# Another order of column tiles and of the steps that run beside them in a hybrid block of pooling, gated DeltaNet, latent attention and MLP

## The chip, the core and the metric

The kernel runs on one core of a Trainium2 chip. Its time is device microseconds of one execution; the kernel before took 1226.1, 1227.61 and 1230.46 us in three runs, median 1227.61. A profile was taken of one execution.

## The reference

One block of depth 1 on x of 1024 rows and 1024 columns, all in float32. One projection gives all inputs of three mixers, whose outputs are joined, projected and added to x; an MLP with squared ReLU follows.

```python
h = rms_norm(x, attn_norm[l])
proj = h @ w_in[l]
xa, qkv, z, b, a, c_q, c_kv, k_pe = jnp.split(proj, offsets, axis=-1)
y_a = pool_mixer(xa, ...)         # window means of 2, 4, 8, 16 rows, minus xa, small product per group
y_b = gated_deltanet(qkv, z, b, a, ...)   # 4 heads of 128
y_c = mla_attention(c_q, c_kv, k_pe, ...) # 4 heads, causal softmax
x = x + jnp.concatenate([y_a, y_b, y_c], axis=-1) @ w_out[l]
h = rms_norm(x, mlp_norm[l])
x = x + jnp.square(jax.nn.relu(h @ w_up[l])) @ w_down[l]
```

The change touches the pooling mixer's projection and the DeltaNet. Its queries, keys and values go through a causal convolution of four taps and silu; per chunk of rows a unit lower triangular system is solved, and then a state of 128x128 per head is carried from chunk to chunk:

```python
sol = lax.linalg.triangular_solve(a_strict, rhs, left_side=True, lower=True, unit_diagonal=True)
def step(state, inp):
    u_i, w_i, qd_i, kd_i, at_i, gl_i = inp
    v_new = u_i - jnp.einsum("bhck,bhkv->bhcv", w_i, state)
    o = jnp.einsum("bhck,bhkv->bhcv", qd_i, state) + jnp.einsum("bhij,bhjv->bhiv", at_i, v_new)
    state = state * gl_i[..., None, None] + jnp.einsum("bhck,bhcv->bhkv", kd_i, v_new)
    return state, o
```

## The kernel before, in words

The kernel takes chunks of 128 rows, eight of them. The input projection is cut into column tiles of 128 columns: 0 and 1 feed the pooling mixer, 2 to 5 the queries of the four heads, 6 to 9 the keys, 10 to 13 the values, 14 to 17 the gates. `proj_tile` works a tile in two halves of 512 rows; each half is 24 products of 128x128 by 128x512 (8 slices of the input times 3 terms of a split into a high and a low part, L123 to L125) into one PSUM bank. `tile_order` says whose weights are fetched ahead; the second operand of `load_w` says whether VectorE (`V`) or GpSimd (`G`) makes the low part of the weights (L116).

Everything else of the DeltaNet is written as generators that wait in queues (`side`, `slow`, `ahead`) and are advanced by `pump` once per half tile: n steps of `side`, m of `slow`. What a half tile has left for later (`later`) runs after the next half's products. Instructions are then set in order on each engine by a scheduler with a model of its own, so that the program's order is a wish and the order on an engine is what counts.

The parts of the DeltaNet, with the names that the rows use:
- `conv_silu` (L503 on ScalarE, three L506 and, in second halves, three L508 on VectorE, L512 on ScalarE, L514 on VectorE) is the convolution of a half tile of keys, queries or values.
- `lanes` inverts all 32x32 diagonal blocks of all heads and chunks at once, 128 of them, one in each partition: 31 pairs of L591 and L593 on VectorE, each dependent on the one before. A transposed copy is made by ScalarE (L595), and both go to DRAM (L596, L597), from where they are read back in block form.
- `levels(h)` builds the inverse of each 128x128 system of head h out of 32x32 blocks. It transposes the keys (L524, copies L725), fetches blocks (L741 to L752), and has five steps of eight small products, one for each chunk (`bat`, L758), with a copy behind each (L765 to L778).
- `chains(a, b)` is the recurrence of two heads. A step of a chunk: state products (L818, L819), the rest of the right side on VectorE (L821), the solve (L828), a scaled copy on VectorE (L832), the state's update (L839, then L844 on VectorE), the output (L847, L851). Every four chunks the norm, a scaling on ScalarE (L796), transposes (L801) and the gating (L803).
- The gates are made into `zs` by L716 and L717, the mixer's outputs copied by L657, the values transposed by L704, the products of queries and keys L685 and L688.

Before the change the tiles run: gates 0 and 1, queries 0, values 0, queries 1, values 1, the two mixer tiles, queries 2, values 2, queries 3, values 3, then the first halves of gates 2 and 3 and their second halves beside the first attention work. `lanes` was put in `side` ahead of the gates. `heads(0, 1)` enters `side` after values 1: the levels of two heads in turns, then their recurrence. `heads(2, 3)` enters after values 3.

Of the kernel before, what the change touches and what calls it, by code (L numbers as in the profile page):

```python
# [37 lines left out]
YU = 20  # L38
LAG = 2
OFF = 2  # L40
SIDE = 7
LANE = 4
BANKS = {"mm": 4, "sm": 2, "ch": 2, "s2": 2}
WINDOWS = (2, 4, 8, 16)
# [19 lines left out]
def block_kernel(ctx, tc, x, x_t, params, positions, attn_norm, w_tiles, w_g, w_qb, w_kvb, w_out,  # L64
# [14 lines left out]
    V, A, G, PE = nc.vector, nc.scalar, nc.gpsimd, nc.tensor  # L79
# [365 lines left out]
    def load_w(src, shape=(P, KD, P), eng=None):  # L445
        raw = S(shape, "raw", 3)
        nc.sync.dma_start(raw, src)
        hi, lo = S(shape, "w", 4, F32R), S(shape, "w", 4, F32R)
        split(hi, lo, raw, eng)
        return hi, lo  # L450
# [18 lines left out]
        while slow or side or ahead:  # L469
            pump(1, 1, 1)  # L470

    tile_order = [6, 7, 8, 9, 14, 15, 2, 10, 3, 11, 0, 1, 4, 12, 5, 13, 16, 17]
    loaded = {}

    def prefetch(ct):
        if ct not in loaded:
            loaded[ct] = load_w(w_tiles[ct], eng=V if ct in (15, 2, 10, 3, 11) else G)

    def proj_tile(ct, use, n=0, m=1, halves=(0, 1), tag="mm", between=None):
        prefetch(ct)  # L480
        hi, lo = loaded[ct]
        nxt = tile_order.index(ct) + 1
        for hf in halves:
            if hf == halves[-1] and nxt < len(tile_order):
                prefetch(tile_order[nxt])
            pm = MM(tag)
            due = later[:]
            del later[:]
            for k in range(KD):
                mm3(pm, hi[:, k, :], lo[:, k, :], ht_hi[hf][:, k, :], ht_lo[hf][:, k, :], k == 0, k == KD - 1)  # L490
            use(hf, pm)
            for f in due:
                f()
            pump(n, m)
            if between and hf == halves[0]:
                between()
# [121 lines left out]
    def pool(i, xa):  # L618
        cur = xa
        shifts = (1, 2) if i == 0 else (1, 2, 4, 8)  # L620
        for n, s in enumerate(shifts):
            nxt = U(s="xs")
            rows = slice(0, P) if n < len(shifts) - 1 else slice(64, P)
            if n == len(shifts) - 1:
                A.copy(nxt[0:64, :], cur[0:64, :])
            G.tensor_copy(nxt[rows, 0:s], cur[rows, 0:s])
            G.tensor_tensor(nxt[rows, s:], cur[rows, s:], cur[rows, :1024 - s], op=ALU.add)
            cur = nxt
            yield
        yp = U(s="yp")  # L630
        G.tensor_tensor(cur[:, 0:16], cur[:, 0:16], rcp[:, i, :], op=ALU.mult)
        G.tensor_tensor(yp[:, 0:16], cur[:, 0:16], xa[:, 0:16], op=ALU.subtract)
        V.scalar_tensor_tensor(yp[:, 16:], cur[:, 16:], rw[:, i:i + 1], xa[:, 16:], op0=ALU.mult, op1=ALU.subtract)
        nc.sync.dma_start(y_dram[i], yp)
        yield
# [17 lines left out]
    def mixer(i):  # L653
        xa = XA[i] = U(s="xa")

        def use_x(hf, pm):
            A.copy(xa[:, hf * 512:(hf + 1) * 512], pm)  # L657

        return i, use_x
# [16 lines left out]
    def query_key(h):  # L676
        qt = QT[h]
        transposed(qt, square_sums(ssq[:, h, :]))
        V.tensor_scalar(tq[:, h, :], ssq[:, h, :], EPS, EPS * 128.0, op0=ALU.add, op1=ALU.mult)
        att = E[h]  # L680
        for b in range(2):
            pk = MM("sm")
            for j in range(4):
                c = 4 * b + j
                PE.matmul(pk[:, j * P:(j + 1) * P], KT[h][:, c * P:(c + 1) * P], qt[:, c * P:(c + 1) * P], start=True, stop=True)  # L685
            for j in range(4):
                c = 4 * b + j
                V.scalar_tensor_tensor(att[:, c, :], pk[:, j * P:(j + 1) * P], c2[:, h, c:c + 1], att[:, c, :], op0=ALU.mult, op1=ALU.mult)  # L688

    def values(h):  # L690
        vs = VS[h] = U((P, NC, P), s="vs")
        vt = [None, None]

        def half(hf):
            vt[hf] = W()
            return vt[hf]

        def use_v(hf):
            later.append(lambda: turn_v(hf))

        def turn_v(hf):
            pt = MM("sm")
            for j in range(4):
                PE.transpose(pt[:, j * P:(j + 1) * P], vt[hf][:, j * P:(j + 1) * P], ident)  # L704
            for j in range(4):
                c = 4 * hf + j
                A.activation(vs[:, c, :], pt[:, j * P:(j + 1) * P], AF.Copy, scale=sk[:, h, c:c + 1])

        return 10 + h, conv_silu(8 + h, half, use_v)
# [11 lines left out]
    def levels(h):  # L721
        kk = KK[h] = U((P, NC, P), s="ktok")

        def use_k(b, pt):
            A.copy(kk[:, 4 * b:4 * b + 4, :].rearrange("p a b -> p (a b)"), pt)  # L725

        transposed(KT[h], use_k)
        tt2 = TT2[h] = U((P, NC, P), s="tt2")
        w1, w2, w3 = U((P, 2, NC, 64), s="w1"), U((P, 2, NC, 64), s="w2"), C((64, 2, NC, 32), "lv", 3)
        a_pair, w_pair = w1[0:64, 0], w1[0:64, 1]  # L730
        a_half, t_half, w_half = w2[0:64, 0], w2[0:64, 1], w2[64:128, 0]
        t_even, tt_odd = w3[:, 0], w3[:, 1]
        a_src = a_dram[h].rearrange("j (c i) -> j c i", c=NC)

        def block(q, b):
            return t_dram[q, h * 32 + b * 8:h * 32 + b * 8 + 8].rearrange("c (i j) -> i c j", i=32)

        G.memset(w1[0:64].rearrange("p a b c -> p (a b c)"), 0.0)
        for p_ in range(2):
            rows = slice(32 * p_, 32 * p_ + 32)  # L740
            nc.scalar.dma_start(a_pair[rows, :, rows], a_src[64 * p_:64 * p_ + 32, :, 64 * p_ + 32:64 * p_ + 64])  # L741
            nc.sync.dma_start(t_even[rows], block(0, 2 * p_))
            nc.sync.dma_start(tt_odd[rows], block(1, 2 * p_ + 1))
        G.memset(t_half[0:32, :, 32:64], 0.0)
        nc.scalar.dma_start(a_half, a_src[0:64, :, 64:128])
        for b in range(2):
            rows = slice(32 * b, 32 * b + 32)
            nc.sync.dma_start(t_half[rows, :, rows], block(0, b))
        G.memset(tt2.rearrange("p a b -> p (a b)"), 0.0)
        for b in range(4):  # L750
            rows = slice(32 * b, 32 * b + 32)
            nc.sync.dma_start(tt2[rows, :, rows], block(1, b))  # L752
        yield

        def bat(n, w, lhs, rhs):
            pa = MM(LVB)[0:n, 0:NC * w].rearrange("p (a b) -> p a b", a=NC)
            for c in range(NC):
                PE.matmul(pa[:, c, :], lhs[:, c, :], rhs[:, c, :], start=True, stop=True)  # L758
            return pa


        pa = bat(64, 32, a_pair, t_even)
        for p_ in range(2):
            rows = slice(32 * p_, 32 * p_ + 32)
            A.activation(w_pair[rows, :, rows], pa[rows], AF.Copy, scale=-1.0)  # L765
        yield
        pa = bat(32, 32, tt_odd[0:32], w_pair[0:32, :, 0:32])
        A.copy(t_half[32:64, :, 0:32], pa)
        yield
        pa = bat(64, 32, w_pair, tt_odd)  # L770
        for p_ in range(2):
            A.copy(tt2[64 * p_:64 * p_ + 32, :, 64 * p_ + 32:64 * p_ + 64], pa[32 * p_:32 * p_ + 32])
        yield
        pa = bat(64, 64, a_half, t_half)
        A.activation(w_half, pa, AF.Copy, scale=-1.0)
        yield
        pa = bat(64, 64, w_half, tt2[64:128, :, 64:128])
        V.tensor_copy(tt2[0:64, :, 64:128], pa)  # L778
        yield
        if h == 1:  # L780
            tap("TT2", tt2.rearrange("p a b -> p (a b)"))
# [82 lines left out]
                split(Y[2 + h][b][:, 0, :], Y[2 + h][b][:, 1, :], QT[h][:, 512 * b:512 * b + 512], YENG)  # L864
                yield

    def heads(*hs):
        gens = [levels(h) for h in hs]
        while gens:
            for g in list(gens):  # L870
                try:
                    next(g)
                    yield
                except StopIteration:
                    gens.remove(g)
        yield from chains(*hs)

    dn_half = const((P, 1), "dn_half")
    V.tensor_scalar(dn_half, pv("dn_norm"), 0.5, None, op0=ALU.mult)
    for h in range(2):  # L880
        proj_tile(*gate(h), LANE, 2)
        if h == 0:
            later.append(key_scales)
    for h in range(H):
        n = LANE if h < 2 else SIDE
        queries(h, n)
        proj_tile(*values(h), n, between=lambda: later.append(lambda: query_key(h)))
        if h == 1:
            drain()
            side.append(heads(0, 1))  # L890
            for i in range(2):
                proj_tile(*mixer(i), SIDE, 3)
                slow.append(pool(i, XA[i]))
    side.append(heads(2, 3))
    ends = [gate(h) for h in (2, 3)]
    for z in ends:
        proj_tile(*z, SIDE, halves=(0,))
# [409 lines left out]
    n = 0  # L1307
# [266 lines left out]
```

## Time and profile before

| | |
|---|---|
| median of three runs | 1227.61 us (1226.1 to 1230.46) |
| profiled execution | 1227.87 us |
| its span from the first to the last instruction | 1226.2 us |
| PE (products) busy | 1174.1 us, 96% |
| DVE (VectorE) busy | 849.6 us, 69% |
| ACT (ScalarE) busy | 582.1 us, 47% |
| POOL (GpSimd) busy | 266.7 us, 22% |
| mean granted clock of TensorE | 0.976 |

Busy time is the time in which at least one instruction of the engine ran; matmuls are pipelined, so that a matmul with a duration of 0.39 us is followed by the next after 0.227 us. The granted clock is the share of full speed that TensorE was given: 1.00 is 2.4 GHz and 0.50 is 1.2 GHz; a mean over a window between these says that both levels occurred in it.

### The profile page before, as it was taken

The numbers are of one execution on the slowest core, as the hardware profiler recorded it, in microseconds if no ns is written. First come the engines' busy times: TensorE is split into PE (matmuls) and PEld (weight loads), VectorE is DVE, ScalarE is ACT, GpSimd is POOL, SyncE is SP. The second block draws the span as 40 slices with busy tenths as digits, with TensorE's granted clock in tenths as the row PEclk, the third lists the DMA queues.
The fourth block names the chain that finished last, engine by engine and source line by source line (L and its number), as shares of the span: only waits on it lengthen the run. The fifth ranks groups of instructions, "written<-read, shape, count | busy, mean of one in ns | idle before, by whom it ended". The sixth has DMA issues, their size and how long they took to land.

```text
span 1226.2 us, 16233 instructions
## 1 busy us (share of the span) xinstructions
PE 1174.1 (96%) x5802; PEld 968.5 (79%) x5802; DVE 849.6 (69%) x1484; ACT 582.1 (47%) x1220; POOL 266.7 (22%) x309
## 2 busy tenths in 40 slices
PE   5999999899999889999899999999999999999998
PEld 5967777787778678788687788888888888888887
DVE  7676649627835877537698767667669897786863
ACT  6455434434644677524265455454554433333330
POOL 0135540232220326200423423424310000000000
PEclk9999999979998989999799999999999999999999
DMA  6101331320121211462125443443469964443302
GB/s 258 56 31 74 125 112 39 87 53 31 54 51 43 78 36 35 141 254 89 67 69 189 163 153 139 163 156 145 155 248 356 350 221 156 136 137 103 102 26 96
DMA packets 85696, 152.60 MB, mean 124 GB/s; under 512 B 25456, under 2 KB 28656, under 8 KB 85616
## 3 DMA queue, kind: packets, MB, share of 16 engines
q1 hardware_dynamic: 76624, 144.23, 33.3%
q10 hardware_dynamic: 8992, 7.34, 1.9%
q8 instruction: 46, 0.75, 0.2%
q14 instruction: 34, 0.28, 0.1%
HBM read 105.41 MB, written 46.14 MB: 124 GB/s over the span
## 4 chain that ended last, share of the span: by engine, by line
PE 75%; DVE 14%; ACT 4%; issue 3%; POOL 2%; DMA 1%; SPq 0%; DVEq 0%; ACTq 0%; POOLq 0%
PE mm L1449 14%; PE mm L1205 12%; PE sm L1205 6%; PE ch L1449 5%; PE sm L1449 5%; PE mm L125 4%; PE mm L124 4%; PE mm L123 4%; PE ch L1205 3%; DVE t2k L506 2%; PE sm L758 2%; PE ch L125 1%; DVE wop L116 1%; PE ch L123 1%; PE ch L124 1%
## 5 line engine op out<-in xcount | busy, mean ns | idle before, releaser
L1449 PE MATMUL mm<-dop,dop 128*128 128x512 f32 x768 | 176.0, 389 | 0.0
L1449 PEld LDWEIGHTS mm<-dop,dop 128*128 128x128 f32 x768 | 144.2, 188 | 29.9
L1205 PE MATMUL mm<-H,wop 128*128 128x512 f32 x576 | 141.5, 398 | 3.3 <-DVE uo L1273 2.7
L1205 PEld LDWEIGHTS mm<-H,wop 128*128 128x128 f32 x576 | 110.1, 192 | 28.1 <-DVE uo L1273 3.7
L115 ACT CAST dop<-wdr 128x1024 fp32r<-128x1024 f32 x48 | 50.4, 1050 | 151.2 <-PE mm L1449 62.9
L123 PE MATMUL mm<-H,w 128*128 128x512 f32 x288 | 118.7, 412 | 2.5 <-DVE zs L717 2.5
L125 PE MATMUL mm<-H,w 128*128 128x512 f32 x288 | 117.6, 408 | 0.0
L124 PE MATMUL mm<-H,w 128*128 128x512 f32 x288 | 117.3, 407 | 0.0
L1205 PE MATMUL sm<-op,wop 128*128 128x512 f32 x384 | 92.4, 389 | 1.4 <-ACT p L1271 1.4
L1205 PEld LDWEIGHTS sm<-op,wop 128*128 128x128 f32 x384 | 72.0, 188 | 16.8 <-ACT p L1271 1.9
L116 DVE TENSOR_TENSOR dop<-wdr,dop 128x1024 fp32r<-128x1024 f32 x48 | 58.6, 1222 | 31.2 <-ACT dop L115 31.2
L1295 ACT ACTIVATE uo<-uo 128x512 f32<-128x512 f32 x48 | 30.3, 631 | 98.3 <-DVE uo L1273 56.5
L1242 POOL TENSOR_TENSOR s<-upr 128x512 f32<-128x512 f32 x16 | 25.7, 1605 | 217.2 <-DVE uo L1231 98.2
L1449 PE MATMUL sm<-dop,dop 128*128 128x512 f32 x288 | 67.4, 389 | 0.0
L1449 PE MATMUL ch<-dop,dop 128*128 128x512 f32 x288 | 67.4, 389 | 0.0
L116 POOL TENSOR_TENSOR w<-raw,w 128x1024 fp32r<-128x1024 f32 x13 | 31.9, 2453 | 158.4 <-ACT w L115 158.4
L116 DVE TENSOR_TENSOR wop<-s,wop 128x512 fp32r<-128x512 f32 x64 | 45.7, 729 | 29.3 <-ACT wop L115 29.3
L123 PEld LDWEIGHTS mm<-H,w 128*128 128x128 f32 x288 | 55.5, 193 | 11.9 <-DVE zs L717 2.9
L506 DVE SCALAR_TENSOR_TENSOR t2k<-mm,cw,t2k 128x511 f32<-128x511 f32 (+2 forms) x72 | 53.5, 743 | 15.4 <-ACT t2k L503 15.1
L125 PEld LDWEIGHTS mm<-H,w 128*128 128x128 f32 x288 | 55.4, 192 | 10.1
L116 DVE TENSOR_TENSOR dop<-H,dop 128x1024 fp32r<-128x1024 f32 x52 | 63.2, 1216 | 0.0
L124 PEld LDWEIGHTS mm<-H,w 128*128 128x128 f32 x288 | 55.7, 193 | 9.3
(390 smaller groups left out, 2644.7 us busy)
## 6 DMA issues: line engine op xcount, KB each, us to landing
H<-u_dram SPq DMA_DIRECT2D x52, 512.0 KB, 4.3
upr<-in_w_up_dram SPq DMA_DIRECT2D x38, 512.0 KB, 4.0
u_dram<-t SPq DMA_DIRECT2D x64, 256.0 KB, 2.0
wdr<-in_w_down_dram SPq DMA_DIRECT2D x32, 512.0 KB, 7.7
u_dram<-uo SPq DMA_DIRECT2D x48, 256.0 KB, 2.0
raw<-in_w_tiles_dram SPq DMA_DIRECT2D x18, 512.0 KB, 3.4
wor<-in_w_out_dram SPq DMA_DIRECT2D x10, 512.0 KB, 8.4
x<-in_x_dram SPq DMA_DIRECT2D x8, 512.0 KB, 3.5
```

Source lines behind the costliest of these rows:

```text
L115: A.copy(hi, src)
L116: (eng or V).tensor_tensor(lo, src, f32(hi), op=ALU.subtract)
L123: PE.matmul(o, ah, bh, start=first, stop=False)
L124: PE.matmul(o, ah, bl, start=False, stop=False)
L125: PE.matmul(o, al, bh, start=False, stop=last)
L506: V.scalar_tensor_tensor(acc[:, s:], pm[:, :512 - s], w, acc[:, s:], op0=ALU.mult, op1=ALU.add)
L758: PE.matmul(pa[:, c, :], lhs[:, c, :], rhs[:, c, :], start=True, stop=True)
L1205: PE.matmul(o, x_, y_, start=(first and j == 0 and q == 0), stop=(j == 3 and q == 2), skip_group_check=True)
L1242: G.tensor_tensor(v.s12[:, 0], a21, a22, op=ALU.add)
L1295: A.activation(o, o, AF.Relu)
L1449: PE.matmul(o, x_[:, cs_], y_, start=(q in (0, 1, 3) and i == 0 and e == 0), stop=(i == GP - 1 and e == 2), skip_group_check=True)
```

## The change

The two mixer tiles move in front of queries 0, right behind gates 0 and 1, with `lanes` beside them; after them the program finishes what is left of `lanes`. Their weights are now split on VectorE. `heads` goes: `blocks` runs the levels one head after the other, and the recurrence is queued by itself. `blocks(0, 1)` is in `side` during queries and values 0 and 1, two steps per half tile; `chains(0, 1)` and `blocks(2, 3)` during queries and values 2 and 3; `chains(2, 3)` after those. `SIDE`, the steps per half tile from queries 2 on, is 8 for 7.

```diff
-SIDE = 7
+SIDE = 8
-    tile_order = [6, 7, 8, 9, 14, 15, 2, 10, 3, 11, 0, 1, 4, 12, 5, 13, 16, 17]
+    tile_order = [6, 7, 8, 9, 14, 15, 0, 1, 2, 10, 3, 11, 4, 12, 5, 13, 16, 17]
-            loaded[ct] = load_w(w_tiles[ct], eng=V if ct in (15, 2, 10, 3, 11) else G)
+            loaded[ct] = load_w(w_tiles[ct], eng=V if ct in (15, 0, 1, 2, 10, 3, 11) else G)
-    def heads(*hs):
-        gens = [levels(h) for h in hs]
-        while gens:
-            for g in list(gens):
-                try:
-                    next(g)
-                    yield
-                except StopIteration:
-                    gens.remove(g)
-        yield from chains(*hs)
+    def blocks(*hs):
+        for h in hs:
+            yield from levels(h)
...
+    for i in range(2):
+        proj_tile(*mixer(i), LANE, 2)
+    while side:
+        step(side, 1)
+    side.append(blocks(0, 1))
     for h in range(H):
-        n = LANE if h < 2 else SIDE
+        n = 2 if h < 2 else SIDE
         queries(h, n)
-        proj_tile(*values(h), n, between=lambda: later.append(lambda: query_key(h)))
+        proj_tile(*values(h), n, 3, between=lambda: later.append(lambda: query_key(h)))
         if h == 1:
             drain()
-            side.append(heads(0, 1))
-            for i in range(2):
-                proj_tile(*mixer(i), SIDE, 3)
-                slow.append(pool(i, XA[i]))
-    side.append(heads(2, 3))
+            side.append(chains(0, 1))
+            side.append(blocks(2, 3))
+            slow.extend(pool(i, XA[i]) for i in range(2))
+    side.append(chains(2, 3))
```

How this moves the engines' orders is shown at three places. On VectorE, the lanes. Before, early in queries 0 (the two tiles `mm_` are halves of queries 0):

```order
L591 TENSOR_TENSOR lt_1813<-lanes_741,tl_1807 128x87
L508 SCALAR_TENSOR_TENSOR t2k_2030<-carry_1956,cw,t2k_2030 128x1
L593 TENSOR_TENSOR tl_1807<-tl_1807,lt_1813 128x29x3
L506 SCALAR_TENSOR_TENSOR t2k_2030<-mm_2005,cw,t2k_2030 128x510
L591 TENSOR_TENSOR lt_1813<-lanes_741,tl_1807 128x112
L508 SCALAR_TENSOR_TENSOR t2k_2030<-carry_1956,cw,t2k_2030 128x2
L593 TENSOR_TENSOR tl_1807<-tl_1807,lt_1813 128x28x4
```

After, the same pairs, which now stand beside the mixer's tiles:

```order
L591 TENSOR_TENSOR lt_1813<-lanes_741,tl_1807 128x87
L593 TENSOR_TENSOR tl_1807<-tl_1807,lt_1813 128x29x3
L591 TENSOR_TENSOR lt_1813<-lanes_741,tl_1807 128x112
L593 TENSOR_TENSOR tl_1807<-tl_1807,lt_1813 128x28x4
L591 TENSOR_TENSOR lt_1813<-lanes_741,tl_1807 128x135
L593 TENSOR_TENSOR tl_1807<-tl_1807,lt_1813 128x27x5
```

The convolutions between the pairs are gone; the first one of queries 0 now stands behind 43 of the 62 lane instructions.

On TensorE, the block products of heads 0 and 1. Before, in the second half of the second mixer tile (`mm_2772`; the `sm_` tiles are outputs of `bat`, of two heads in turns, and the last row is the first product of the recurrence):

```order
L758 MATMUL sm_2534<-lv_2506,w_408_2504 64x32 x8
L758 MATMUL sm_2545<-w_401_2471,lv_2473 32x32 x8
L124 MATMUL mm_2772<-H_101,w_2578 128x512
L125 MATMUL mm_2772<-H_99,w_2579 128x512
L758 MATMUL sm_2555<-w_408_2504,lv_2506 32x32 x8
L758 MATMUL sm_2565<-lv_2473,w_401_2471 64x32 x8
L758 MATMUL sm_2608<-lv_2506,w_408_2504 64x32 x8
L123 MATMUL mm_2772<-H_99,w_2578 128x512
L758 MATMUL sm_2619<-w_402_2472 64x64 x8
L758 MATMUL sm_2629<-w_409_2505 64x64 x8
L758 MATMUL sm_2639<-tt_400_2470,w_402_2472 64x64 x8
L758 MATMUL sm_2649<-tt_407_2503,w_409_2505 64x64 x8
```

After, head 0 alone, in the first half of queries 1 (`mm_2449`):

```order
L758 MATMUL sm_2175<-lv_2158,w_340_2156 64x32 x8
L124 MATMUL mm_2449<-H_100,w_2308 128x512
L125 MATMUL mm_2449<-H_98,w_2309 128x512
L123 MATMUL mm_2449<-H_98,w_2308 128x512
L124 MATMUL mm_2449<-H_100,w_2308 128x512
L125 MATMUL mm_2449<-H_98,w_2309 128x512
L123 MATMUL mm_2449<-H_98,w_2308 128x512
L758 MATMUL sm_2228<-w_340_2156,lv_2158 32x32 x8
L758 MATMUL sm_2238<-lv_2158,w_340_2156 64x32 x8
L758 MATMUL sm_2286<-w_341_2157 64x64 x8
L124 MATMUL mm_2449<-H_100,w_2308 128x512
```

The five steps of head 0 stand four and more half tiles earlier in the row of tiles, with 6 and 9 matmuls between them; the fifth follows in the second half of queries 1.

On TensorE, the start of the second recurrence. Before, the last block products of heads 2 and 3 and c0 stand early in a second half of a gate tile (`mm_3905`), with a whole half tile behind it:

```order
L758 MATMUL sm_3818<-tt_693_3653,w_695_3655 64x64 x8
L758 MATMUL sm_3828<-tt_700_3686,w_702_3688 64x64 x8
L828 MATMUL ch_3841<-vs_3063,tt_693_3653 128x128
...
L818 MATMUL ch_3891<-st_3866,kt_1235 128x128
L819 MATMUL ch_3891<-st_3866,qt_2851 128x128
L818 MATMUL ch_3898<-st_3875,kt_1488 128x128
L819 MATMUL ch_3898<-st_3875,qt_3312 128x128
L123 MATMUL mm_3905<-H_99,w_3500 128x512
L124 MATMUL mm_3905<-H_101,w_3500 128x512
L125 MATMUL mm_3905<-H_99,w_3501 128x512
```

After, head 3's last block product stands in the last half tile (`mm_4211`), whose last matmul comes after c1 (L914 and L925 are the attention's transposes, L917 and L928 in the kernel before):

```order
L758 MATMUL sm_3800<-tt_697_3693,w_699_3695 64x64 x8
...
L828 MATMUL ch_3819<-vs_3433,tt_697_3693 128x128
...
L818 MATMUL ch_3871<-st_3827,kt_1235 128x128
L819 MATMUL ch_3871<-st_3827,qt_2709 128x128
L925 MATMUL sm_4106<-ident,t2k_4104 96x128 x2
L914 MATMUL sm_4138<-ident,raw_4135 96x128
L818 MATMUL ch_3878<-st_3836,kt_1488 128x128
L819 MATMUL ch_3878<-st_3836,qt_3227 128x128
L914 MATMUL sm_4138<-ident,raw_4135 96x128 x3
L125 MATMUL mm_4211<-H_99,w_3729 128x512
```

Behind c1 stand 33 matmuls of the gates' tiles before, and one after.

## Rows read from the trace of the kernel before

**Rows 1.** The page: busy us (share of the span) and instructions.

```profile
PE 1174.1 (96%) x5802; PEld 968.5 (79%) x5802; DVE 849.6 (69%) x1484; ACT 582.1 (47%) x1220; POOL 266.7 (22%) x309
```

**Rows 2.** Windows: length, busy PE, PEld, DVE, ACT, POOL, granted clock, DMA share, GB/s.

```profile
200.00:220.00 20.00, 19.90 (x98) 16.34 (x97) 19.33 (x52) 7.96 (x24) 2.40 (x1) 1.00 0.08 27
220.00:240.00 20.00, 16.11 (x81) 13.38 (x80) 13.65 (x36) 9.52 (x28) 4.50 (x4) 0.91 0.36 102
...
400.00:420.00 20.00, 17.80 (x111) 14.30 (x111) 17.78 (x50) 15.91 (x57) 7.42 (x16) 1.00 0.19 62
420.00:440.00 20.00, 13.44 (x60) 9.42 (x58) 12.52 (x34) 11.88 (x34) 3.93 (x3) 0.74 0.22 73
```

**Rows 3.** Waits of PE, 160 to 450 us: us in total, times, longest.

```profile
PE ch L801 <- ACT lv L796: 5.8, 2, 3.8
PE sm L704 <- DVE t2k L514: 4.6, 2, 3.9
...
PE ch L847 <- DVE st L844: 1.5, 3, 1.0
...
PE sm L685 <- ACT junk L541: 0.6, 1, 0.6
```

**Rows 4.** Short windows in which the clock is low, columns as in rows 2.

```profile
232.00:236.00 4.00, 4.00 (x16) 3.20 (x14) 1.31 (x3) 3.20 (x16) 0.00 (x0) 0.66 0.37 57
254.00:256.00 2.00, 2.00 (x31) 2.00 (x30) 0.00 (x0) 1.05 (x3) 0.00 (x0) 0.80 0.00 0
256.00:260.00 4.00, 4.00 (x33) 3.50 (x33) 0.00 (x0) 1.90 (x4) 2.03 (x2) 0.50 0.02 4
...
268.00:270.00 2.00, 2.00 (x10) 1.66 (x10) 0.19 (x1) 0.00 (x0) 0.00 (x0) 0.78 0.11 45
...
376.00:380.00 4.00, 4.00 (x24) 3.75 (x23) 2.48 (x8) 1.97 (x6) 0.00 (x0) 0.74 0.26 79
```

**Rows 5.** Timeline of PE, at 170 and 381 us: start, length, instruction.

```profile
170.09 0.80 PE L123 MATMUL mm<-H,w 128*128 128x512 f32 x1 [2.48 <-DVE zs L717]
...
172.40 0.63 PE L125 MATMUL mm<-H,w 128*128 128x512 f32 x1
...
380.59 0.38 PE L818 MATMUL ch<-st,kt 128*128 128x128 f32 x2
380.81 0.39 PE L819 MATMUL ch<-st,qt 128*128 128x128 f32 x2
```

**Rows 6.** All L591 (min/median/max ns); timeline of DVE and POOL beside splits.

```profile
L591 DVE TENSOR_TENSOR lt<-lanes,tl x31: 185/358/2372, 184.8 to 226.5; 128x31 f32<-128x31 f32 x2, 128x60 f32<-128x60 f32 x2, 128x87 f32<-128x87 f32 x2, 128x112 f32<-128x112 f32 x2
...
210.85 2.37 DVE L591 TENSOR_TENSOR lt<-lanes,tl 128x247 f32<-128x247 f32 x1
...
210.55 2.40 POOL L116 TENSOR_TENSOR w<-raw,w 128x1024 fp32r<-128x1024 f32 x1 [30.42 <-ACT w L115]
...
222.23 1.85 DVE L593 TENSOR_TENSOR tl<-tl,lt 128x156 f32<-128x156 f32 x1
```

**Rows 7.** Timeline of ACT and SP behind the lanes; last row L741's.

```profile
226.99 1.97 ACT L595 COPY tlt<-tl 128x1024 f32<-128x1024 f32 x1 [5.63 <-DVE tl L593]
...
229.57 1.06 SPq L742 DMA_DIRECT2D lv<-t_dram  x2
...
241.52 0.62 ACT L725 COPY ktok<-sm 128x512 f32<-128x512 f32 x1
...
242.36 0.61 ACTq L741 DMA_DIRECT2D w<-a_dram  x1
...
DMA to landing us min/median/max: 2.1/2.1/2.1
```

**Rows 8.** Timeline of PE: part of the fifth block products of heads 0 and 1.

```profile
260.45 3.30 PE L758 MATMUL sm<-tt,w 64*64 64x64 f32 x29
```

**Rows 9.** The window from c1 to the last transposes, and one group of matmuls, 380 to 430.

```profile
380.60:428.20 47.60, 41.29 (x267) 34.43 (x265) 36.53 (x107) 30.68 (x107) 10.10 (x18) 1.00 0.21 70
...
L123 PE MATMUL mm<-H,w 128*128 128x512 f32 x11 | 4.8, 440 | 0.0
```

## The prediction

> **What bounds the kernel now.** I read the page first, then the 20 us windows, then who waited for whom on TensorE, then short windows where the clock is low, then the timeline around the places that the change touches. The page has PE busy for 1174 of 1226.2 us and DVE for 850 [rows 1]: PE is the bound of the whole, but not of every stretch, and the windows show which ones. Between 160 and 440 us the busy time of PE drops to 16.1 of 20 us at 220 to 240, to 17.8 at 400 to 420 and 13.4 at 420 to 440, and the granted clock falls to 0.91 and 0.74 in windows of low load [rows 2] and to 0.50 between, where PE is never idle [rows 4]. All of the change lies between 170 and 428 us. What follows is placed after it, with one product of queries and keys behind the last transposes as the only difference, so what counts is how much sooner or later the last transposes of the second recurrence (L801, at 428.2 us, where the window of [rows 9] ends) come. I split this at the first state product of the second recurrence, c1 (L818 at 380.6 us [rows 5]), since ahead of it PE sets the pace and behind it the recurrence does.
>
> Before c1, from 170.1 us on, PE waits: L704 behind DVE for 4.6 us, 3.9 of it in one wait; L685 0.6; L801 2.0 (5.8 less the 3.8 of the tail); L847 about 1.4; in all 8.6 us [rows 3]. DVE causes the largest: it is busy 19.3 of 20 us just before [rows 2], with lane inversions and convolutions in turn. The clock costs (1 - clock) x length: 228 to 236 us 0.3 + 1.4 = 1.7; 254 to 270 us 0.4 + 6.0 + 0.4 = 6.8, the 12 us between at 0.50; 366 to 380 us 0.1 + 4.0 + 1.0 = 5.1, eight of them at 0.50 [rows 4]; in all 13.6 us. The second and third are where the block products of two heads stand in one run: 64 records of 64x64 end there, at 0.114 us each (the 29 of [rows 8] take 3.30).
>
> **The change part by part.** *Order of the tiles.* The four half tiles of the mixer go ahead of the first queries and take nothing from the total: 24 matmuls at 0.227 us each, wherever they stand. In front of c1 the scheduler now puts 575 of these matmuls (in full widths) where 546 stood, 29 x 0.227 = +6.6 us. Their place behind c1 is in the time of a recurrence that they did not bound, so nothing comes back for them there.
>
> *Lanes.* Before, the 62 lane instructions are shared out over 42 us, from 184.8 to 226.9 us, with convolutions of the queries and values between them. Now the mixer gives DVE nothing, and they run nearly in one piece. Their durations are 24.4 us, of which two are inflated while a split runs on POOL (2.37 and 1.85 us where the median is 0.36 [rows 6]); as no such split stands beside them now, 20.9. Add 62 x 0.03 us from one to the next, two splits of 1.2, two gate products of 0.7 and the convolutions that the order puts between (some 5.3), less overlap at 14 places of 0.09: 30.6 us. Started at 184.8 again, they end near 215.4 us, 11.5 us sooner. The wait of 3.9 us (L704) and the one of 0.7 go, as the values' products stand behind the lanes' end.
>
> *A new wait at the first block product.* PE meets it after 202 matmuls (45.8 us) and eight transposes of 0.11, started at 170.1 with the eight slow ones that stand there (0.43 for 0.227, 1.6 us [rows 5]); 0.8 us of the transposes goes into the 2.5 us idle ahead of 170.1. That is 170.1 + 45.8 + 0.9 + 1.6 - 0.8 = 217.6 us. The product needs the lanes' matrix back from DRAM and a block that ScalarE's queue fetches. SP: lanes' end to L742's issue 2.6 us, the second issue 0.5 on, and to landing as long as the next, 2.1: ready 5.2 us behind the lanes. ScalarE: L595 2.0, two copies of keys 0.6 each, L741 twice, 0.6 apart, with 2.1 us to landing [rows 7]: 0.1 + 2.0 + 1.2 + 0.6 + 2.1 = 6.0. So ready at 221.4, and PE waits 3.8 us; behind the waiting product stand all later matmuls of queries and values 1, and DVE is busy with older convolutions, so nothing else is late. After 3.9 us idle the trace shows 1.7 us lost to the clock, which I add: 5.5 us. Bounds: 1.5 (PE 2 us later, landing 0.3 sooner) and 9 (a convolution more ahead of the lanes' end).
>
> *Block products head by head.* The five of a head now stand in one or two tiles each, with 6 and 9 matmuls between them; only three stand in a row. The low clock of 254 to 270 and 366 to 380 should then go. Bounds: nothing, and 11.9 us (it falls as before). I take 0.7, since the window from 400 to 420 us, with 111 mostly small products and 2 us idle, is at 1.00 [rows 2].
>
> *Recurrence of heads 0 and 1.* It starts one tile later in the row of tiles, beside queries and values 2 and 3. Its waits, 3.4 us before, I carry at 4.4 (bounds 1 and 8), as more convolutions meet it. SIDE of 8 for 7 and the lower count of 2 only set how many steps the program hands out per half tile; their effect is in the order that I counted.
>
> *Recurrence of heads 2 and 3.* Before, c1 has 33 matmuls of the gates' tiles and the attention's first products beside it [rows 9]; after, one matmul, since head 3's block products now stand in the last half tile. From the first products of a recurrence, c0, to c1 I add 1.0, and 1.0 for small waits not named. From c1 to the last transposes before: 47.6 us, PE busy 41.3, DVE 36.5 [rows 9]. After, DVE's instructions by the order and the same durations are 36.8 us, PE's work about 22. DVE and the hops between three engines set it, and both stay: 47.9. I add 0.7 for a clock that may fall for parts of it, and 0.2 for the product that moves behind the end. Bounds: 45 and 56.
>
> **Sum.** Ahead of c1: -8.6 - 13.6 + 6.6 - 0.8 + 5.5 + 0.7 + 4.4 + 1.0 + 1.0 = -3.8. Behind it: +0.3 + 0.7 + 0.2 = +1.2. Together -2.6 us. The profiled execution took 1227.87 us, 1.67 more than its span and 0.26 more than the median of the three runs, 1227.61; I set the sum against the median: 1225.0 us. A measurement of this kernel can tell 0.3%, 3.7 us, from no change; the forecast is inside.
>
> **A rule against the change.** From 420 to 440 us PE is busy 13.4 of 20 us at a clock of 0.74; from 400 to 420 with 17.8 it is at 1.00 [rows 2]. The Trainium skill, "TensorE: Matmul & The Clock Gate", in its section on HAM oscillation, says that a stream with short bursts between waits falls back to the half clock again and again. No run here yet shows a recurrence with so little beside it. By the row of 400 to 420 the stretch behind c1 stays near 48 us; by that rule it is the rival that ends slower.
>
> **Rivals.** *Clearly faster.* The wait at the first block product is at its lower bound of 1.5 with no clock behind it, the recurrence keeps its 3.4, and the terms of 0.7, 1.0 and 1.0 are nothing: -16.4 + 4.9 + 0.5 = -11 us, 1216.6. For it speaks that two thirds of the 22 us removed is lost clock whose cause goes; against it that DVE's total is untouched.
>
> *Slower: the second recurrence without cover.* Its place is from c1 to the last transposes. PE has 22 us of work in 48, and seven steps of 20 passes each; a pass is 0.11 us at full clock (the second pair of passes starts 0.22 behind the first [rows 5]) and 0.22 at half. On the path lies half of these or all: 7 x 20 x 0.1 = 14, half 7 us; the 22 us of attention work doubles in the gaps. With +9 the stretch takes 57 us and the time is 1225.0 + 9 - 0.7 = 1233.3. It decides from a stretch of 55 us. For it: 13.4 busy goes with 0.74 [rows 2]; against it: DVE's work of 36.8 us must be done at any clock, and part of PE's delay hides behind it.
>
> *The new wait takes the place of the old one in full.* If the lanes end at 219 (the convolutions of the first queries come in between, as before), PE waits 7.4 and loses 2 more with the clock: +4 on the forecast, 1229.0. For it: DVE was busy 19.3 of 20 us here; against it: the order puts 43 of the 62 lane instructions ahead of the first convolution.
>
> *The low clock at the block products stays.* They keep 5 of the 11.9 us: 1229.3. Against it: they stand between matmuls now.
>
> **How the numbers follow.** Forecast 0.46, itself from 1219 to 1230 us; clearly faster 0.24; uncovered recurrence 0.16; the long wait 0.08; the low clock 0.06. The forecast's case lies within 0.3% in 6 of 10 and faster in 4 of 10; the fast rival is faster in 0.23 of 0.24; the uncovered recurrence is slower in 0.13 of 0.16; the last two are within in 0.10 of 0.14 and slower in the rest. Faster: 0.18 + 0.23 = 0.41; slower: 0.13 + 0.04 + 0.01 = 0.18; the same: 0.41. The range reaches over the fast rival's main part and the uncovered recurrence: 1214 to 1234.
>
> **What would show it.** Right: the clock at 1.00 over all block products; one new wait of 2 to 6 us at L758 near 218 us, and none at L704 near 226; lanes ending near 215; c1 some 4 us sooner; from c1 to the last transposes 46 to 50 us. Wrong: a low clock in the last stretch, or waits of DVE in the first recurrence that add to over 8 us.

## The result: 1.05% slower, and the profile after

The changed kernel takes 1241.05 us (1237.82 to 1244.72, 4 runs) against 1229.03 (1226.1 to 1230.71, 4 runs): a ratio of 1.0105, 95% interval 1.0085 to 1.0124. The profiled execution spans 1239.8 us, 13.6 more than before. The first state product of the second recurrence, c1, comes at 390.6 us, 10.0 later than before; from there to the last transposes it is 49.3 us, 1.7 more; the rest is 799.9, 1.9 more. So most of the loss lies where I had forecast a gain of 3.8 us.

Windows of the kernel after, columns as in [rows 2]:

```profile
220.00:240.00 20.00, 18.75 (x121) 15.45 (x121) 8.23 (x15) 7.81 (x24) 0.00 (x0) 0.66 0.30 61
240.00:260.00 20.00, 20.00 (x158) 16.17 (x158) 12.81 (x27) 10.11 (x26) 2.38 (x1) 1.00 0.13 38
260.00:280.00 20.00, 16.84 (x86) 13.64 (x85) 11.70 (x23) 8.47 (x31) 6.39 (x5) 0.91 0.08 26
300.00:320.00 20.00, 16.66 (x90) 14.20 (x89) 15.77 (x40) 11.44 (x45) 8.11 (x7) 0.83 0.13 47
...
360.00:380.00 20.00, 20.00 (x164) 16.37 (x164) 2.91 (x5) 5.63 (x12) 0.00 (x0) 1.00 0.30 69
```

The low clock of before at 360 to 380 us is gone. In its place there is one at 220 to 240 us, and two more at 260 to 280 and 300 to 320 where PE is idle for over 3 us of 20. Waits of PE, 160 to 470 us, as in [rows 3]:

```profile
PE sm L685 <- ACT junk L541: 7.5, 3, 3.3
PE ch L801 <- ACT lv L796: 3.7, 1, 3.7
PE sm L758 <- DMA w<-a_dram: 3.4, 1, 3.4
```

L704 is no longer among them; L758, the first block product, is, and L685, the product of queries and keys, has gone from 0.6 to 7.5 us. The first block product in the timeline:

```profile
221.25 1.88 PE L758 MATMUL sm<-lv,w 64*64 64x32 f32 x16 [3.42 <-DMA w<-a_dram]
```

In short windows behind it:

```profile
222.00:234.00 12.00, 12.00 (x73) 10.03 (x73) 3.21 (x7) 3.62 (x8) 0.00 (x0) 0.50 0.39 83
234.00:236.00 2.00, 2.00 (x23) 1.56 (x22) 0.40 (x2) 0.00 (x0) 0.00 (x0) 1.00 0.00 0
```

The wait is the one forecast (3.8 us near 218). But behind it the clock is at 0.50 for 12 us, 6.0 us lost, with 0.8 just ahead (0.79 from 218 to 222 us), where the wait of 3.9 us of before cost 1.7. Then the timeline of VectorE and GpSimd (start, length) at the convolution of the second half of values 1:

```profile
264.50 1.19 DVE L508 SCALAR_TENSOR_TENSOR t2k<-carry,cw,t2k 128x1 f32<-128x1 f32 x1
265.62 0.73 DVE L506 SCALAR_TENSOR_TENSOR t2k<-mm,cw,t2k 128x510 f32<-128x510 f32 x1
266.28 1.40 DVE L508 SCALAR_TENSOR_TENSOR t2k<-carry,cw,t2k 128x2 f32<-128x2 f32 x1
267.60 0.73 DVE L506 SCALAR_TENSOR_TENSOR t2k<-mm,cw,t2k 128x509 f32<-128x509 f32 x1
268.26 1.51 DVE L508 SCALAR_TENSOR_TENSOR t2k<-carry,cw,t2k 128x3 f32<-128x3 f32 x1
...
263.30 2.39 POOL L116 TENSOR_TENSOR w<-raw,w 128x1024 fp32r<-128x1024 f32 x1 [12.32 <-PE sm L524]
...
265.77 1.89 POOL L627 TENSOR_TENSOR xs<-xa 128x1023 f32<-128x1023 f32 x1
...
267.86 1.89 POOL L627 TENSOR_TENSOR xs<-xs 64x1022 f32<-64x1022 f32 x1
```

L508 adds one to three columns and takes 0.21 us in the median; here it ends each time where GpSimd's instruction ends, after 1.2 to 1.5 us. L506 between them, 510 columns with one operand in PSUM, is not held up. What that does to ScalarE and PE:

```profile
269.80 0.63 ACT L512 ACTIVATE t2k<-t2k 128x512 f32<-128x512 f32 x1 [3.11 <-DVE t2k L508]
270.34 0.26 ACT L541 ACTIVATE junk<-sm 128x128 bf16<-128x128 f32 x1
...
271.54 1.86 PE L685 MATMUL sm<-qt,kt 128*128 128x128 f32 x7 [3.12 <-ACT junk L541]
```

In ScalarE's order L512 stands ahead of the last three of the square sums L541: it waits for L508, they start behind it, and L685 needs the bank that they read. So three held-up sums of one to three columns stop TensorE for 3.12 us. The same comes again at 310 us (3.30), at the second half of values 2. There a second path runs beside it, as ScalarE also waits for the window sum itself:

```profile
310.22 1.04 ACT L625 COPY xs<-xs 64x1024 f32<-64x1024 f32 x1 [2.16 <-POOL xs L627]
```

The kernel before has one such meeting too, at the second half of values 2 (a window sum runs from 310.14 to 312.50 us):

```profile
310.66 1.87 DVE L508 SCALAR_TENSOR_TENSOR t2k<-carry,cw,t2k 128x2 f32<-128x2 f32 x1
```

It cost PE no wait over 1 us there. What the change adds is that all three L508 of a half tile are held, at two places.

### The profile page after: what moved, and what is told of

Same layout as the page of the kernel before. It is cut to its first block, busy times and chain, and to the rows that moved or that the text cites. A ratio compares the mean times of both kernels' runs of the same rounds, so it can differ in the third digit from the quotient of the medians.

```text
span 1239.8 us, 16227 instructions
## 1 busy us (share of the span) xinstructions
PE 1175.7 (95%) x5802; PEld 965.1 (78%) x5802; DVE 858.1 (69%) x1486; ACT 580.9 (47%) x1220; POOL 261.6 (21%) x307
## 4 chain that ended last, share of the span: by engine, by line
PE 71%; DVE 14%; ACT 5%; issue 4%; POOL 3%; DMA 2%; SPq 0%; DVEq 0%; ACTq 0%; POOLq 0%
PE mm L1446 14%; PE mm L1202 12%; PE sm L1202 6%; PE ch L1446 5%; PE sm L1446 5%; PE mm L124 4%; PE mm L125 4%; PE mm L123 4%; PE ch L1202 3%; PE sm L758 2%; DVE t2k L506 2%; PE ch L125 1%; DVE wop L116 1%; PE ch L123 1%; PE ch L124 1%
## 5 line engine op out<-in xcount | busy, mean ns | idle before, releaser
L115 ACT CAST dop<-wdr 128x1024 fp32r<-128x1024 f32 x48 | 50.4, 1050 | 150.7 <-PE mm L1446 62.9
L506 DVE SCALAR_TENSOR_TENSOR t2k<-mm,cw,t2k 128x511 f32<-128x511 f32 (+2 forms) x72 | 53.5, 742 | 19.4 <-ACT t2k L503 18.9
L123 PEld LDWEIGHTS mm<-H,w 128*128 128x128 f32 x288 | 55.4, 192 | 11.4 <-ACT xa L657 1.9
L125 PEld LDWEIGHTS mm<-H,w 128*128 128x128 f32 x288 | 55.3, 192 | 10.0
L1446 PEld LDWEIGHTS ch<-dop,dop 128*128 128x128 f32 x288 | 54.1, 188 | 11.2
L1446 PEld LDWEIGHTS sm<-dop,dop 128*128 128x128 f32 x288 | 54.0, 188 | 11.2
```

The lines of the kernel that those rows point to most:

```text
L115: A.copy(hi, src)
L123: PE.matmul(o, ah, bh, start=first, stop=False)
L125: PE.matmul(o, al, bh, start=False, stop=last)
L506: V.scalar_tensor_tensor(acc[:, s:], pm[:, :512 - s], w, acc[:, s:], op0=ALU.mult, op1=ALU.add)
L1446: PE.matmul(o, x_[:, cs_], y_, start=(q in (0, 1, 3) and i == 0 and e == 0), stop=(i == GP - 1 and e == 2), skip_group_check=True)
```

## The experiments

Theory A: GpSimd's window sums, which now stand beside the convolutions of the second halves of values 1 and 2, hold up L508 and through it L685. Theory B: the wait at the first block product, and the half clock behind it. Theory C: the second recurrence without cover. Each row below gives the median of its runs with the ratio to the kernel before (its medians on the chips used: 1229.1, 1229.3 and 1229.8), and from the profile, in us: c1, the time from c1 to the last transposes, PE's idle time from 166 us to c1, and the clock lost there, (1 - clock) x length, good to about 1 us since the clock has two decimals. The profile is of one execution, which can lie up to 3.7 us from the median of its kernel (f3_carry_pool).

| kernel | us | ratio, 95% | c1 | to the end | idle | clock |
|---|---|---|---|---|---|---|
| before | 1229.0 | 1 | 380.6 | 47.6 | 11.1 | 15.0 |
| after | 1241.1 | 1.0105 (1.0085 to 1.0124) | 390.6 | 49.3 | 16.2 | 11.2 |
| e1_pool_late | 1235.7 | 1.0052 (1.0030 to 1.0073) | 381.2 | 53.0 | 11.0 | 4.3 |
| e2_blocks_late | 1242.9 | 1.0104 (1.0062 to 1.0147) | 392.8 | 47.9 | 15.6 | 15.9 |
| e4_before_seq | 1225.8 | 0.9962 (0.9946 to 0.9978) | 375.7 | 47.7 | 10.7 | 2.1 |
| e5_carry_act | 1230.3 | 1.0013 (0.9996 to 1.0030) | 378.5 | 49.8 | 8.4 | 4.2 |
| f1_seq_carry | 1237.5 | 1.0073 (1.0046 to 1.0100) | 386.6 | 52.2 | 14.2 | 11.0 |
| f3_carry_pool | 1230.2 | 1.0007 (0.9988 to 1.0026) | 379.3 | 53.0 | 7.3 | 10.7 |
| f4_short_lanes | 1235.5 | 1.0055 (1.0034 to 1.0076) | 385.1 | 50.1 | 12.8 | 8.8 |
| f5_mixer_first_seq | 1246.3 | 1.0147 (1.0107 to 1.0187) | 398.5 | 50.4 | 18.4 | 16.3 |
| g6_no_sums | 1232.6 | 1.0016 (0.9998 to 1.0034) | 383.4 | 49.5 | 10.1 | 10.9 |
| h1_no_sums_short | 1222.6 | 0.9947 (0.9929 to 0.9966) | 371.9 | 48.7 | 6.8 | 0.0 |
| h3_seq_side8 | 1226.2 | 0.9973 (0.9958 to 0.9989) | 376.1 | 47.2 | 8.4 | 4.2 |
| g2_seq_split | 1224.4 | 0.9955 (0.9935 to 0.9975) | 377.6 | 48.1 | 10.7 | 4.2 |

c1 less idle and clock is 354.5 us before and 361 to 366 in all others: the matmuls that now stand ahead of c1. What tells the kernels apart is idle and clock, and the last stretch.

**Undoing parts.** e1_pool_late:

```diff
-            slow.extend(pool(i, XA[i]) for i in range(2))
+    slow.extend(pool(i, XA[i]) for i in range(2))     # behind values 3
     side.append(chains(2, 3))
```

> The changed kernel with the pooling steps queued behind values 3 instead of behind values 1, all else as in it. Theory A (GpSimd's window sums L627 beside the second halves of queries 2 and values 2 hold up VectorE's short L508, and with them ScalarE and the products L685): the two waits of PE at L685 near 268 and 310 us (3.1 and 3.3 us) and the low clock behind them go, 8 to 11 us less than the changed kernel, about 1231 us. Theory B (the loss comes from the wait at the first block product and the half clock behind it, the rest is noise): less than 2 us changes. Theory C (the thin cover of the second recurrence): as late or later, since the sums now stand beside it.

Measured 5 us less than the changed kernel, for the 8 to 11 expected. Ahead of c1 theory A holds: idle and clock fall by 12 us, the clock at 260 to 280 and 300 to 320 us is at 1.00, and c1 comes 9.4 sooner; 3.7 are given back behind c1, where the sums now stand beside the second recurrence and the clock is at 0.81 over all of it:

```profile
381.20:434.10 52.90, 40.47 (x224) 33.46 (x222) 36.88 (x106) 29.07 (x105) 17.07 (x27) 0.81 0.23 76
```

e2_blocks_late:

```diff
-        n = 2 if h < 2 else SIDE
+        n = (0, LANE, SIDE, SIDE)[h]
```

> The changed kernel with the block products of heads 0 and 1 started one pair of tiles later (no steps beside queries 0 and values 0, four beside queries 1 and values 1). Theory B: the wait of 3.4 us at L758 near 218 us and the half clock from 222 to 234 us go, 7 to 9 us less than the changed kernel, about 1233 us. Theory A: the waits at L685 stay, and only the 3.4 us wait goes, at most 4 us less. If the half clock follows the block products themselves and not the wait, it comes again beside them later, and the gain is 3 us.

No gain: the lanes still end at the same time, and PE waits as long for the values' convolution behind them.

```profile
220.60 1.12 PE L704 MATMUL sm<-ident,t2k 128*128 128x128 f32 x4 [3.98 <-DVE t2k L514]
```

After this wait the clock is back at 1.00 from 228 us, but it falls again from 256 to 268 us (0.50 from 258 to 266) beside the block products of head 1, with no wait ahead of them. So thin products can pull the clock down by themselves; the expectation's third case comes nearest, without its gain.

e4_before_seq:

```diff
     def heads(*hs):
-        gens = [levels(h) for h in hs]
-        while gens:
-            ...
+        for h in hs:
+            yield from levels(h)
         yield from chains(*hs)
```

> The kernel before with one part of the change alone: the block products of two heads one head after the other instead of in turns. If the low clock of before at 254 to 270 and 366 to 380 us comes from two heads' products in one run, it goes or halves there: up to 11.9 us less clock loss. Theory C: the products of head 3 end a half tile later, the second recurrence loses its 33 matmuls of cover, and from c1 to the last transposes it takes 2 to 8 us longer; the sum between 5 us faster and 5 us slower than the kernel before. Theory A has no part here: within 2 us.

This part alone makes the kernel before 0.38% faster. The clock is at 1.00 over all block products:

```profile
240.00:260.00 20.00, 20.00 (x164) 16.41 (x163) 1.03 (x2) 8.61 (x18) 7.63 (x7) 1.00 0.25 57
260.00:280.00 20.00, 19.94 (x160) 16.68 (x159) 10.99 (x28) 8.86 (x27) 10.61 (x11) 1.00 0.16 54
360.00:380.00 20.00, 19.71 (x169) 16.38 (x167) 7.46 (x19) 9.13 (x25) 0.00 (x0) 1.00 0.34 93
```

12.9 us of clock come back. Some 12 of them are in the three windows shown, where the block products stood; 1.8 are at 160 to 180 us (0.91 before, 1.00 here), ahead of all that the edit moves, and are not its doing: that window is at 0.91 again in h3_seq_side8 and g2_seq_split. 8.4 us of work (c1 less idle and clock, 362.9 for 354.5) move ahead of c1, and c1 is 4.9 us sooner. Behind c1 nothing is lost (47.7 for 47.6), although only two matmuls are left there: theory C falls for this size of cover. The other parts of the change therefore cost 15 us.

e5_carry_act:

```diff
-                if hf:
+                if hf and 4 <= ci < 8:             # keys as before
                     V.scalar_tensor_tensor(acc[:, :s], carry[:, 3 - s:], w, acc[:, :s], ...)
+            for s in (1, 2, 3) if hf and not 4 <= ci < 8 else ():
+                for j in range(s):
+                    A.activation(acc[:, j:j + 1], carry[:, 3 - s + j:4 - s + j], AF.Identity, bias=acc[:, j:j + 1], scale=cw[:, ci, 3 - s:4 - s])
```

> The changed kernel with the short carry products L508 of queries and values made by ScalarE, six one-column instructions per second half, instead of three by VectorE. Theory A in its narrow form (VectorE's L508 with two operands from SBUF waits for the end of a GpSimd instruction): the 1.2 to 1.9 us instructions go, the three L506 run at 0.74 each, the waits at L685 near 268 and 310 us shrink to under 1 us each in spite of about 1.2 us more on ScalarE; 4 to 9 us less than the changed kernel. If VectorE is late for another reason (its order, or ScalarE's), no gain, or up to 3 us slower.

10.8 us less than the changed kernel, more than the 4 to 9 expected, with the sums left where they are. This speaks for theory A in the narrow form, but not all of it is theory A: the order moved too, the wait at the first block product is 2.2 us for 3.4, and the clock at 220 to 240 us is 0.74 for 0.66. No wait at L685 is among the first of the list any more.

```profile
PE ch L804 <- ACT lv L799: 3.7, 1, 3.7
PE ch L842 <- DVE st L847: 2.5, 3, 1.4
PE sm L761 <- DMA w<-a_dram: 2.2, 1, 2.2
PE ch L821 <- ACT ot L826: 2.1, 1, 2.1
```

(Lines here are three higher: L761 is the block product, L804 the transposes.)

**Parts combined.** f1_seq_carry is e4_before_seq with e5_carry_act's edit.

> The kernel before with the block products head by head (3 us faster by itself) and the carry products L508 of queries and values on ScalarE. VectorE's long L508 of that kernel (1.2 to 2.4 us beside GpSimd's splits at 282, 301 and 341 us) go; the waits of before at L704 near 226 us (lanes) stay. If L508 costs where GpSimd is busy only, 1 to 3 us less than with the head by head order alone, about 1224 us; if more ScalarE work ahead of L512 costs as much, no gain.

A miss: 11.7 us slower than the head by head order alone. Idle rises by 3.5 us and lost clock by 8.9 ahead of c1, and the last stretch takes 52.2 us. The six instructions also changed the order on all engines (the products of queries and keys of head 1 stand 10 matmuls later and more), so that this run can't say which of the two costs this. g2_seq_split, below, has the products of head 1 at the same places of TensorE's row (10 and 12 matmuls later) and isn't slower, so that this shift alone isn't it. The waits that grew are L704's near 231 us (4.5 us for 3.9) and one of the transposes L524 near 247 us for VectorE's L688 (2.5 us, 0.4 in g2_seq_split). Why they grew stays open, and e5_carry_act by itself is no clean proof.

f3_carry_pool is the changed kernel with both remedies, e1_pool_late's and e5_carry_act's.

> The changed kernel with both remedies: carry products on ScalarE and the pooling steps behind values 3. If both remedy the same loss (GpSimd's sums beside L508), they don't add: as the carry products alone, about 1230 us, within 3 us; later by 2 to 4 us if the sums beside the second recurrence cost something by themselves (with them there PE waited 1.4 and 2.3 us near 379 and 385 us). If they remedy two losses, about 1225 us.

As e5_carry_act alone: this fits one loss, remedied twice, and not two.

f5_mixer_first_seq is e4_before_seq with the tile order, the mixer's place and the weights split on VectorE of the change; `heads` and the pooling steps are queued behind values 1.

> The kernel before with the block products head by head, and the tile order of the change: the mixer's tiles first with the lanes beside them; the recurrence of heads 0 and 1 with its block products still starts behind values 1, so now beside queries 2, and the pooling steps are queued there. If the tile order alone loses what the changed kernel loses, 1238 to 1243 us. By its parts: the wait of 3.9 us at L704 stays but no block products follow it (less clock lost), GpSimd's sums stand beside second halves of queries and values 2 and 3 as in the changed kernel (8 to 11 us), and the first recurrence starts four half tiles later than in the kernel before, so the second starts with no tile left beside it: 1236 to 1246 us.

The tile order with block products that stay late is 17 us over the kernel before, no better than the whole change. By the medians, pulling the block products of heads 0 and 1 forward gained some 5 us of this, but that isn't shown: the intervals of the two kernels overlap, and the steps per half tile differ as well.

**Leaving work out.** g6_no_sums leaves out the window sums; the order on each engine is the same as in the changed kernel, row by row.

```diff
-            G.tensor_tensor(nxt[rows, s:], cur[rows, s:], cur[rows, :1024 - s], op=ALU.add)
+            G.memset(nxt[rows, s:], 0.0)
```

> The changed kernel with GpSimd's six window sums (L627) left out, each replaced by a memset of the same tile; the order on every engine is the same. A memset of 128x1024 takes 0.95 us on GpSimd where the sum took 1.9, and reads nothing. Theory A in its narrow form: L508 beside it takes 0.21 us and not 1.2 to 1.9; the waits at L685 near 268 and 310 us (3.1 and 3.3 us) and the half clock behind them (1.7 and 3.4 us) go but for a part due to the splits of weights beside L508; c1 8 to 10 us sooner, 7 to 10 us less than the changed kernel, about 1233 us. If VectorE is held up by its own order, nothing changes.

8.5 us less. At the place shown above, the timeline now reads:

```profile
264.59 1.19 DVE L508 SCALAR_TENSOR_TENSOR t2k<-carry,cw,t2k 128x1 f32<-128x1 f32 x1
...
266.36 0.20 DVE L508 SCALAR_TENSOR_TENSOR t2k<-carry,cw,t2k 128x2 f32<-128x2 f32 x1
...
267.15 0.20 DVE L508 SCALAR_TENSOR_TENSOR t2k<-carry,cw,t2k 128x3 f32<-128x3 f32 x1
...
265.83 1.97 POOL L627 MEMSET xs<- 128x1023 f32 x2
```

And among its waits of PE:

```profile
PE sm L685 <- ACT junk L541: 2.7, 3, 1.1
```

Beside the memsets L508 takes 0.20 us; beside the split of weights, which is unchanged, still 1.19. The waits at L685 shrink from 7.5 to 2.7 us. Since no order changed, this shows theory A: the sums hold up L508, and that costs the waits at L685. The low clock at 260 to 280 and 300 to 320 us goes with them (both windows at 1.00). The idle time ahead of c1 falls by 6.1 us and c1 comes 7.2 sooner. The clock lost ahead of c1 hardly falls in this execution (10.9 us for 11.2), since it drops at another place, beside the block products of head 3, where the changed kernel had 1.00:

```profile
360.00:380.00 20.00, 20.00 (x154) 16.01 (x154) 4.00 (x7) 6.58 (x16) 0.00 (x0) 0.85 0.16 41
```

No run here shows why.

f4_short_lanes leaves out the last 15 of the 31 pairs of lane instructions of the changed kernel:

```diff
+            if j >= 16:
+                yield
+                continue
             V.tensor_tensor(tv, L[:, j, j + 1:32].unsqueeze(2)...
```

> The changed kernel with the last 15 of the 31 pairs of lane instructions left out, so that the lanes end some 8 us sooner. Theory B: the wait of 3.4 us at the first block product goes, and with it the half clock from 222 to 234 us (6 us lost): 8 to 10 us less than the changed kernel, about 1232 us; part of it may be due to less work on VectorE, whose convolutions of values 0 come sooner. If the half clock comes from the block products and not from the wait, the clock stays low there and the gain is 3 to 4 us.

Theory B holds for its place: the wait goes, and with it all of the half clock.

```profile
220.00:240.00 20.00, 19.95 (x138) 15.81 (x137) 9.52 (x22) 11.03 (x35) 0.00 (x0) 1.00 0.19 47
```

The first state product comes 8.5 us sooner (273.3 for 281.8), but the kernel only 5.6: the waits at L685 (8.3 us in all for 7.5) and a clock under 1 after 360 us (0.90 from 360 to 380) take up a part. VectorE also has 30 instructions less here, so that some of the gain may come from that.

h1_no_sums_short has both left out.

> The changed kernel with both left out: the window sums of the pooling mixer and the last 15 pairs of lane instructions. If the two losses are separate they add: 5.6 us (short lanes, measured) and what the sums alone give, together 13 to 16 us less than the changed kernel, 1225 to 1228 us, the time of the kernel before; what then is left against the head by head order alone (1225.8 us) is the later start and thinner cover of the second recurrence, about 2 us. If the later waits of the sums only take up what the shorter lanes give, no more than the larger of the two, 7 to 10 us.

18.5 us less than the changed kernel, for 8.5 and 5.6 by themselves; the 4.4 us between are no more than the four intervals leave open (each about 2.4 us to either side). In the profiled execution no clock at all is lost ahead of c1. The time is no longer than e4_before_seq's (3.2 us under it, with overlapping intervals), so theories A and B are enough for the loss, and theory C has at most the 1 us by which the last stretch is longer (48.7 for 47.7; 49.3 in the changed kernel). Less work was done in this kernel, which is why its time is no goal.

**Towards a better kernel.** h3_seq_side8 is e4_before_seq with `SIDE = 8`; g2_seq_split is e4_before_seq with tiles 0 and 1 in the list that VectorE splits.

> The kernel before with the block products head by head and 8 steps per half tile for 7, the two parts of the change that leave the tile order as it was. The products of the first recurrence stand up to 20 matmuls earlier in places and its last transposes 24 earlier; the second recurrence starts at the same place. If head by head is what gains, as measured alone: 3 to 4 us less than the kernel before, 1225.5 us; the 8 steps add between 1 us faster and 1 us slower.

> The kernel before with the block products head by head and the low parts of the mixer tiles' weights made on VectorE, as in the change. The two lane instructions that took 2.4 and 1.9 us beside those splits on GpSimd fall to 0.4 and 0.3 (3.5 us less), VectorE gets two splits of 1.2 (2.4 us more): the wait at L704 near 226 us shrinks by about 1 us, 0 to 2 us less than head by head alone, about 1225 us. The scheduler also moves the block products 11 matmuls later here, which may cost up to 3 us.

Both beat the two kernels of this case, and neither can be told from e4_before_seq: 1226.2 and 1224.4 against 1225.8 us, with overlapping intervals. The head by head order is the part of the change to keep.

## Why the prediction was wrong, point by point

**The step that failed: the pooling steps were not priced.** The prediction looked at GpSimd only beside the lanes, where it saw that a split holds up an instruction of VectorE [rows 6], and concluded that the change removes such meetings. It did remove these: the longest L591 is now 0.43 us and not 2.37. But the diff also queues the pooling steps in another place, behind values 1, and no sentence counted their six sums against what VectorE does there. The clue was in the row: the lane instruction, 0.36 us in the median, ended 0.27 us behind the GpSimd instruction that ran beside it (213.22 and 212.95 us). The Trainium skill, "GPSIMD Engine Reference", section "Specifications", says that GpSimd shares its SBUF interface with VectorE and contends with those of its instructions that have two SBUF inputs. The trace agrees: L508, with both in SBUF, is stretched from 0.21 to 1.2 to 1.5 us; L506, with one in PSUM, stays at 0.73. The price in this kernel: 6.9 us of waits more at L685 and some 5 us of clock behind two of them in the trace; 8.5 us of the time come back without the sums (g6_no_sums), where 2.7 us of these waits remain.

**A new wait at the first block product: mechanism right, the clock behind it mis-sized.** Lanes ended at 213.8 us (forecast 215.4), the wait was 3.4 us (3.8). "After 3.9 us idle the trace shows 1.7 us lost to the clock, which I add" took the price from a wait that full matmuls follow. Here block products follow, and the loss was 6.8 us. With the wait gone (f4_short_lanes), it was none. The window 220 to 240 us of the other runs agrees: 0.91 or 0.83 (1.8 to 3.4 us lost) behind a wait of 3.1 to 4.5 us at L704, which transposes and full matmuls follow (before, e2, e4, f1, f5, h3), and 0.74 or 0.66 (5.2 to 6.8 us) behind a wait of 2.0 to 3.4 us at L758, which block products follow (after, e1, e5, f3, g6). The rule that I held against the last stretch bears on this place only in part: the Trainium skill, "TensorE: Matmul & The Clock Gate", in its section on HAM oscillation, says that short bursts between waits fall back to the half clock. The clock did fall at a wait of 3.4 us; but here it is one wait, and PE was busy 12.00 of the 12 us at 0.50 behind it, so that the length of this low clock isn't explained by the rule.

**Block products head by head: right.** Forecast -11.9 + 0.7 us of clock and +6.6 us of matmuls ahead of c1; measured alone -12 at the block products (-12.9 in all) and +8.4. In the changed kernel this held for heads 1 to 3; head 0's are those behind the new wait.

**Recurrence of heads 0 and 1:** forecast 4.4 us of waits; from 281 to 390 us PE waits 1.5 us once (L818 behind VectorE's L851) and 1.0 us at L524, and the other 4.4 us are L685's.

**Recurrence of heads 2 and 3: right in size.** Forecast 47.9 + 0.7 us, measured 49.3:

```profile
390.60:439.90 49.30, 37.17 (x223) 30.69 (x221) 34.27 (x104) 28.65 (x103) 10.03 (x18) 0.92 0.20 65
```

The clock, by (1 - clock) x length 3.9 us for the 0.7 forecast, did fall here, which the prediction had named as a sign of being wrong, but little of it reached the time. The rival that made this stretch the reason for a slower kernel was wrong about the place. The trace of before has 30 matmuls of the gates' tiles behind c1 and not 33, since the 11 of [rows 9] take in some of those ahead of c1; the term of 29 x 0.227 us stands.

**The sum.** Ahead of c1 the forecast was -3.8, and +10.0 was measured. From 166 us on, idle: forecast 11.1 - 8.6 - 0.8 + 3.8 + 4.4 + 1.0 + 1.0 = 11.9, measured 16.2. Clock: 15.0 - 13.6 + 1.7 + 0.7 = 3.8, measured 11.2. Work: +6.6, measured +8.7. These are 4.3 + 7.4 + 2.1 = 13.8 us, the whole difference. The time lies 7 us above the range, since no rival held a loss by GpSimd, and the rival of the low clock was given 0.06.

## What to carry to other kernels

When a diff moves work between queues, list what moves on every engine and lay each piece beside what the others do there; an engine that is 22% busy can still stop the one that bounds. Where a wait is followed by thin products, its price can be the wait and more clock than behind the same wait ahead of full matmuls (6.8 us for 1.7 here); take the price from a row with the same successor. When a change has parts, run them apart: here one was worth -0.4% and was hidden by two losses that cost more.

## What the runs showed of the hardware that I had not expected

One GpSimd sum of two SBUF operands stretches a VectorE instruction of 0.2 us with two SBUF operands to its own end, up to 1.95 us in this stretch (L508 at 310.79 us); a memset of the same tile by GpSimd does not (0.20 us). And a loss of clock can move instead of going: with the sums or the lanes left out, 11 and 9 us of clock are lost ahead of c1 in the profiled execution, 3 and 2 of them from 360 to 380 us, where the changed kernel is at 1.00; with both left out, none. Whether the times of the two losses add isn't settled by the runs.
